# A streaming-encoder block on one core: turned inputs in alternating banks, weight units behind evictions and sums at two borders, one more warming matmul

## The chip, the cores and the metric

One core of one Trainium2 chip runs the whole program in one launch. The metric is the device time of that launch in microseconds, as the median of several runs.

## The reference

One layer (DEPTH is 1) on 256 tokens of width 1024, all in float32:

```python
x = x + 0.5 * rmsnorm(swiglu(rmsnorm(x, ffn1_pre_g), ffn1_w_in, ffn1_w_down), ffn1_post_g)
h = rmsnorm(x, mix_pre_g)
q_a, f_a, i_a, g_a, q_b, k_b, v_b, f_b, gates = split(h @ w_in)
y_a = (rmsnorm(hgrn2(q_a, f_a, i_a), hg_norm_g) * silu(g_a)) @ w_branch_a   # gated recurrence, 8 heads of 128
y_b = fox_attention(q_b, k_b, v_b, f_b + fox_f_bias) @ w_branch_b           # causal, with forget gates
y = sigmoid(gate_A) * y_a + sigmoid(gate_B) * y_b
x = x + rmsnorm(y @ w_out, mix_post_g)
x = x + rmsnorm(cross_attention(rmsnorm(x, mem_pre_g), rmsnorm(mem, mem_kv_g)) , mem_post_g)   # 4 heads, 256 memory rows
x = x + 0.5 * rmsnorm(swiglu(rmsnorm(x, ffn2_pre_g), ffn2_w_in, ffn2_w_down), ffn2_post_g)
```

`D_FF` is 2816. `rmsnorm(x, g)` is x divided by the root of its mean square, times a gain row.

## The kernel before

**Products in three parts.** Every projection keeps float32 accuracy by splitting both factors into a high part (rounded to the type `fp32r`) and a low part (what is left). A product is then hi times hi, hi times lo and lo times hi, added up in one PSUM bank. A matmul has 128 rows and mostly 512 columns.

**Weights in units.** The weights come from DRAM as units of 128 x 1024 floats (512 KB), in the order of `_ORDER`; `_AT[name] + i` is the number of unit i of a matrix. `unit(name, i)` loads one at its first use through `load_split`: SyncE issues the DMA into one of 4 `raw` buffers, ScalarE casts it to `hi` (L143), VectorE subtracts to get `lo` (L145), each into one of 8 buffers. Four units make one group of 512 columns (`chunk`); in a matrix laid out by rows (`mo`, `f2_dn`) each unit is one block of 128 rows. `place` gives a unit other buffers (named `w` in the profile: units 0 and 1 of `i_a` and of `f2_in`). `hold` names for a unit two instructions, one on ScalarE and one on VectorE: its cast is queued behind the first and its subtraction behind the second.

**The order of work.** The program is written once, in Python; a scheduler then puts each engine's instructions into a fixed queue, in the order of the program, but passing over what its own model says is not ready. Three means bind it: `hold`; `tc.issue_after(instruction)`, which queues what follows behind an instruction of the same engine; and `after(i)`, which puts TensorE work behind the i-th matmul of `log` (all matmuls so far) and ahead of everything else that is ready. Constants such as `L_MO` and `L_F2` are such places, counted from a mark `m = len(log)`.

**Turning.** Before each projection the tokens x (rows are tokens, `xs`, two halves of 128) are turned, so that the width lies on the partitions. `to_T` does this for one half: TensorE transposes eight blocks of 128 x 128 into two PSUM banks (four in each, from the pool `trp` of two banks), and `gain_split` evicts each block twice: ScalarE writes the high part with the gain (`hlT`, L358), VectorE the low part (L359), which needs the high one. `evicted` lists the two instructions of each block. `half` calls `to_T` for one half of the tokens, with all eight blocks at one mark or with four at each of two marks, and then `rstd_x` computes the half's 1/rms from sums of squares.

**After a projection.** `post` takes a half's two accumulators: sums of squares on ScalarE (`ssq`, junk), a reciprocal root in `root`, a scaled copy times the gain row on VectorE (`post`, L399), a refining `step`, and the sum into `xs` (L404).

**The two borders.** At border 1 the first FFN ends: its second half's last matmuls run while the first half is turned (mark `L_F1`), then `i_a`, the first projection of the mixer, starts: first half with column groups 0 and 1, then the second half (turned at `L_IA`). At border 2 the output projection `mo` of the cross-attention ends: `rows_proj(po[0], ...)`, `post(po[0])`, `rows_proj(po[1], ...)`, meanwhile the turning of the first half at `L_MO` and four matmuls later, then `post(po[1])`, and the second FFN starts with column groups 0 and 1 of `f2_in` for the first half; the second half is turned at `L_F2`.

**The start.** `WARM` float32 matmuls of ones by ones run while the first inputs (`head`, `raw`) are on their way; then `act_first` takes two column groups of FFN 1 together, block by block of the width as the inputs land.

**`mem_out`** multiplies the attention weights with the memory's values, two heads' columns at a time, into a bank of `trp`; the other pools of banks are `mm` (two) and `acc` (four).

Of the kernel before, what the change touches and what calls it, by code (L numbers as in the profile page):

```python
# [14 lines left out]
AF = mybir.ActivationFunctionType  # L15
ALU = mybir.AluOpType
AX = mybir.AxisListType

P = 128
# [17 lines left out]
L_F1 = 24  # L37
L_IA = 40
L_WO = 20
L_MK = 76  # L40
L_MO = 19
L_F2 = 36
L_OA = (4, 24)
F_S = 12
# [10 lines left out]

HX = T + 2 * KB

WARM = 7

X_AT = 12  # L60

# [8 lines left out]
_AT = {}  # L70
# [8 lines left out]
def block_kernel(ctx: ExitStack, tc: tile.TileContext, wts, head_in, gf_in, x_in, mem_in, memT_in, cols, rows, fbias, masks, out):  # L79
    nc = tc.nc  # L80
    V, S, G, PE = nc.vector, nc.scalar, nc.gpsimd, nc.tensor
# [21 lines left out]
    def nm(s):  # L103
        count[0] += 1
        return f"{s}_{count[0]}"
# [4 lines left out]
    def s1(n=1, dt=F32, name="s"):  # L110
        return sp.tile([P, n], dt, tag=f"s{n}", name=nm(name), bufs=16)
# [4 lines left out]
    def mm():  # L116
        return pp.tile([P, 512], F32, tag="mm", name=nm("mm"), bufs=2)

    def trp():
        return pp.tile([P, 512], F32, tag="tr", name=nm("tr"), bufs=2)  # L120
# [5 lines left out]
    evicted = []  # L126
    hold = {}
# [121 lines left out]
    ident = cp.tile([P, P], F32, name="ident")  # L249
# [9 lines left out]
    G_F1, G_MIX, G_MEM, G_KV, G_F2, G_HG, C_LB = 0, 8, 16, 24, 32, 40, 48  # L259
# [22 lines left out]
    def ssq(dst, src):  # L282
        S.activation(junk[:, : src.shape[-1]], src, AF.Square, accum_out=dst)  # L283
# [6 lines left out]
    def sums_of(s, pre2=None):  # L290

        b = s1(name="v")
        if pre2 is None:
            V.tensor_scalar(out=b, in0=s[:, 0:1], scalar1=D * EPS, scalar2=None, op0=ALU.add)
        else:
            V.tensor_scalar(out=b, in0=s[:, 0:1], scalar1=pre2, scalar2=D * EPS, op0=ALU.mult, op1=ALU.add)
        return b

    def root(s, b, pre=None, pre2=None):

        sc = 1.0 if pre2 is None else pre2
        y, v = s1(name="y"), s1(name="v")
        S.activation(y, s[:, 1:2], AF.Abs_reciprocal_sqrt, bias=b, scale=sc)
        S.activation(v, s[:, 1:2], AF.Identity, bias=b, scale=sc)
        z = y
        if pre is not None:
            z = s1(name="z")
            S.activation(z, y, AF.Copy, scale=pre)
        return y, v, z

    def step(y, v, z):
# [25 lines left out]
    def fac_of(i, h):  # L337
        return fac[i][:, 32 * h : 32 * h + 1]
# [14 lines left out]
    def gain_split(X, kb, src, g, a=0, b=T, first=False):  # L353
        gs = cols_s[:, g + kb : g + kb + 1] if isinstance(g, int) else g
        if first:
            hi = V.tensor_scalar(out=X.hi(kb, a, b), in0=src, scalar1=gs, scalar2=None, op0=ALU.mult)
        else:
            hi = S.activation(X.hi(kb, a, b), src, AF.Copy, scale=gs)  # L358
        lo = V.scalar_tensor_tensor(out=X.lo(kb, a, b), in0=src, scalar=gs, in1=X.hi(kb, a, b).bitcast(F32), op0=ALU.mult, op1=ALU.subtract)  # L359
        evicted.append((hi.ins, lo.ins))  # L360

    def to_T(X, src, h, g, qs=(0, 1)):

        for q in qs:
            ps = trp()
            for j in range(4):
                kb = 4 * q + j
                PE.transpose(ps[:, j * P : (j + 1) * P], src(kb), ident)  # L368
            for j in range(4):
                gain_split(X, 4 * q + j, ps[:, j * P : (j + 1) * P], g, h * P, h * P + P)  # L370

    def x_blocks(h):
        return lambda kb: xs[:, h, kb * P : (kb + 1) * P]
# [5 lines left out]
    def load_row(i):  # L379
        r = m4([P, D], n="grow")  # L380
        nc.sync.dma_start(r, rows[i].partition_broadcast(P))
        return r

    def post(ps, h, grow, factor=1.0, pre=None, cuts=((0, 512), (512, 1024)), store=False):

        pre2 = None
        if pre is not None:
            pre2 = s1(name="pre2")
            V.tensor_tensor(out=pre2, in0=pre, in1=pre, op=ALU.mult)
        s = s1(2, name="ss2")  # L390
        ts = []
        for j in range(2):
            ssq(s[:, j : j + 1], ps[j])
            if j == 0:
                b = sums_of(s, pre2)
            else:
                y = root(s, b, pre, pre2)
            t = sp.tile([P, 512], F32, tag="z2", name=nm("post"), bufs=3)
            V.scalar_tensor_tensor(out=t, in0=ps[j], scalar=-factor * 16.0, in1=grow[:, j * 512 : (j + 1) * 512], op0=ALU.mult, op1=ALU.mult)  # L399
            ts.append(t)  # L400
        r = step(*y)
        for a, b in cuts:
            xh = xs[:, h, a:b]
            V.scalar_tensor_tensor(out=xh, in0=ts[a // 512][:, a % 512 : (b - 1) % 512 + 1], scalar=r, in1=xh, op0=ALU.mult, op1=ALU.add)  # L404
            if store:
                (nc.scalar if a in (320, 768) else nc.sync).dma_start(out[h * P : (h + 1) * P, a:b], xh)


    def ffn(w_in, w_dn, X, r2, n_tok, i_row, first_half, second_half=None):
# [77 lines left out]
        for h in range(2):  # L487
            m = len(log)
# [5 lines left out]
        accs = None  # L494
        done = 0
        if callable(r2):
            outs = act_first((0, 1), acc)
            r2 = r2()
# [6 lines left out]
        for c in range(n_tok, NFF):  # L505
# [13 lines left out]
            if c == 6:  # L519
                grow = load_row(i_row)  # L520
# [3 lines left out]
            if accs is None:  # L524
                accs = [[acc(), acc()], [acc(), acc()]]
# [8 lines left out]
        m = len(log)  # L534
# [4 lines left out]
        m = len(log)  # L539
        if first_half:  # L540
            for c in range(NFF - STAG, NFF):
                down(c, 1)
            first_half(m)
            post(accs[1], 1, grow, 0.5, r2[1])
        else:
            for cut in (left, right):
                for c in range(NFF - STAG, NFF):
                    down(c, 1, (cut,))
            post(accs[1], 1, grow, 0.5, r2[1], ((0, 320), (320, 512), (512, 768), (768, 1024)), True)
# [4 lines left out]
    X1 = Joined()  # L554
    heads, raw1 = [], []
    for kb in range(KB):
# [7 lines left out]
        if kb % 2 == 0 or kb == 1:  # L564
            a, b = ((0, 512), (512, D))[kb] if kb < 2 else (0, D)
# [4 lines left out]
    one = nc.const_aps.tensor(1.0, (P, P), F32)  # L570
    for _ in range(WARM):
        MM(wps[:, :P], one, one, start=True, stop=True)
# [23 lines left out]
    X2 = Joined()  # L596
    r2 = [None, None]

    def half(X, r, h, g, *ms, into=None, act=True):

        for i, m in enumerate(ms):
            with after(m):
                to_T(X, x_blocks(h), h, g, (i,) if len(ms) == 2 else (0, 1))
        r[h] = rstd_x(x_halves(h), into, act)

    ffn("f1_in", "f1_dn", X1, norm_1, 0, 0, lambda m: half(X2, r2, 0, G_MIX, m + L_F1, into=fac_of(0, 0)))


    for i in range(2):
# [2 lines left out]
    for h in range(2):  # L612
        m = len(log)
        for c in range(2):
            ps = mm()
            if h == 0 and c == 1:
                for i in range(4):
                    hold[_AT["i_a"] + 4 + i] = evicted[-1 if i else -3]
            u = chunk("i_a", c)
            proj_tok(ps, X2, u, h)  # L620
            iv_last = S.activation(iv[c][:, h, :], ps, AF.Copy, scale=r2[h]).ins
        if h == 0:
            half(X2, r2, 1, G_MIX, m + L_IA, into=fac_of(0, 1))
# [25 lines left out]
    for c in range(2):  # L649
        u = chunk("f_a", c)  # L650
        f, k = m4([P, 2, 4, P], n="f"), m4([P, 2, 4, P], n="k")
        for j in range(2):
            fj = heads_of(f, j)
            for i in (2 * j, 2 * j + 1):
                ps = acc()
# [10 lines left out]
    for c in range(2):  # L666
        u = chunk("q_a", c)
        q = m4([P, 2, 4, P], n="q")
        for j in range(2):
            qj = heads_of(q, j)  # L670
            z = sp.tile([P, 2, 2, P], F32, tag="z2", name=nm("z2"), bufs=3)
            for i in range(2):
                ps = acc()
# [162 lines left out]
    for c in range(3):  # L836
        u = [load_split(gf_in[4 * c + i], GF) for i in range(4)]
        n = min(GF, D - c * GF)
        for h in range(2):
            ps = mm()  # L840
# [33 lines left out]
    for c in range(2):  # L874
        for name, lst, sc in (("k_b", kb_, 1.0), ("q_b", qb_, 1.0 / math.sqrt(128.0))):
            u = chunk(name, c)
            t = m4([P, 4, T], n=name)
            m = len(log)
            for j in range(2):
                if c == 0:  # L880
                    ps = proj_col2(X2, u, (2 * j, 2 * j + 1))
                else:
                    for i, bank in enumerate((mm, trp)):
                        ps = bank()
                        proj_both(ps, X2, u, 2 * j + i)
                        added(t[:, 2 * j + i], ps)
                    ps = t[:, 2 * j : 2 * j + 2]
# [32 lines left out]
    for h in range(2):  # L920
        ps = [acc(), acc()]
        for hd in range(8):
            g, i = hd // 4, hd % 4
# [5 lines left out]
        r = rstd_x(ps)  # L929
# [80 lines left out]
    m = len(log)  # L1010
    for c in range(2):
        u = chunk("v_b", c)
        t = m4([P, 2, 512], n="v_b")
        for h in range(2):
            ps = mm()
# [23 lines left out]
    m = len(log)  # L1039
# [43 lines left out]
    for c in range(2):  # L1083
        for name, X, zc in (("br_a", OA, c), ("br_b", OB, 2 + c)):
            u = chunk(name, c)
            for h in range(2):
                z = zs[zc][:, h]
                m = len(log)
                ps = mm()
# [21 lines left out]
    po = [[acc(), acc()], [acc(), acc()]]  # L1111
    m = len(log)
# [6 lines left out]
    m = len(log)  # L1119
# [5 lines left out]
    m = len(log)  # L1125
    for c in range(2):
        u = chunk("mk", c)
        KM.more()
        for j in range(2):
            js = slice(2 * j, 2 * j + 2)  # L1130
            t = sp.tile([P, 2, T], F32, tag="z2", name=nm("km"), bufs=3)
            for i in range(2):
                ps = acc()
# [6 lines left out]
    for c in range(2):  # L1140
        u = chunk("mq", c)
        QM.more()
        for i in range(4):
            ps = acc()
# [18 lines left out]
    m = len(log)  # L1163
# [39 lines left out]
    g3 = load_row(2)  # L1203
    AO = Pair()

    def mem_out(i):
        ps = trp()
        for j in range(2):
            o = ps[:, j * T : (j + 1) * T]
            for sb in range(2):  # L1210

                n = sb * 512 + (2 * (i % 2) + j) * P
                vh = VM.h[i // 2][:, n // T, n % T : n % T + P]
                vl = VM.l[i // 2][:, n // T, n % T : n % T + P]
                MM(o, vh, pT.h[sb][:, i], start=(sb == 0), stop=False)
                MM(o, vl, pT.h[sb][:, i], start=False, stop=False)
                MM(o, vh, pT.l[sb][:, i], start=False, stop=(sb == 1))
        i2 = slice(2 * (i % 2), 2 * (i % 2) + 2)
        marks[2 + i] = split(AO.h[i // 2][:, i2], AO.l[i // 2][:, i2], ps.rearrange("p (a t) -> p a t", a=2))
# [8 lines left out]
    for i in range(2, 4):  # L1228
        mem_out(i)
# [7 lines left out]
    po = [[acc(), acc()], [acc(), acc()]]  # L1237
# [2 lines left out]
            rows_proj(po[h], AO, "mo", h, (kb,))  # L1240
    for n in range(2):
        rows_proj(po[0], AO, "mo", 0, range(3, KB), (n,))
    post(po[0], 0, g3)
    m = len(log)
    rows_proj(po[1], AO, "mo", 1, range(3, KB))
    half(X4, r4, 0, G_F2, m + L_MO, m + L_MO + 4, into=fac_of(3, 0))
    post(po[1], 1, g3)


# [95 lines left out]
```

## Time and profile before

| | |
|---|---|
| median of 3 runs | 786.16 us (785.62 to 787.29) |
| the profiled execution | 788.36 us, of which its span is 786.1 us |
| TensorE (PE) busy | 777.3 us, 99% |
| VectorE (DVE) busy | 555.4 us, 71% |
| ScalarE (ACT) busy | 462.8 us, 59% |
| GpSimd (POOL) busy | 15.7 us, 2% |
| DMA | 148.08 MB, mean 188 GB/s |

How to read it: times count from the span's start. A row of the timeline is: start, length, engine, line, operation, what is written from what, shapes, how many merged into the row, and in brackets the idle time before it with what ended that. A row of waits is: who waited for whom, total us, times, longest. A row of the windows view is: stretch, its length, then for PE, PEld, DVE, ACT and POOL the busy time and the number of instructions, then the granted TensorE clock, the DMA share and GB/s. PE is TensorE's matmuls (their ends are modelled), PEld its weight loads; a tile's name stands without its number.

### The profile page before, as it was taken

The numbers are of one execution on the slowest core, as the hardware profiler recorded it, in microseconds if no ns is written. First come the engines' busy times: TensorE is split into PE (matmuls) and PEld (weight loads), VectorE is DVE, ScalarE is ACT, GpSimd is POOL, SyncE is SP. The second block draws the span as 40 slices with busy tenths as digits, with TensorE's granted clock in tenths as the row PEclk, the third lists the DMA queues.
The fourth block names the chain that finished last, engine by engine and source line by source line (L and its number), as shares of the span: only waits on it lengthen the run. The fifth ranks groups of instructions, "written<-read, shape, count | busy, mean of one in ns | idle before, by whom it ended". The sixth has DMA issues, their size and how long they took to land.

```text
span 786.1 us, 12160 instructions
## 1 busy us (share of the span) xinstructions
PE 777.3 (99%) x4620; PEld 669.9 (85%) x4620; DVE 555.4 (71%) x895; ACT 462.8 (59%) x777; POOL 15.7 (2%) x39
## 2 busy tenths in 40 slices
PE   9999999999999999999999999999999999999996
PEld 7888888888888999898888888888887888888885
DVE  7766665586778899588676666885588566655563
ACT  7664544566765668467676345753667554544552
POOL 0000000000000102100000000000000000000000
PEclk9999999999999999999999999999999999999999
DMA  9665665463654546734576655465174546665431
GB/s 347 245 223 202 228 211 207 161 211 125 216 205 145 181 135 208 276 122 152 183 263 226 215 181 168 148 207 181 54 263 166 166 163 203 217 211 199 161 108 53
DMA packets 44505, 148.08 MB, mean 188 GB/s; under 512 B 5144, under 2 KB 8864, under 8 KB 44448
## 3 DMA queue, kind: packets, MB, share of 16 engines
q1 hardware_dynamic: 43168, 144.83, 53.5%
q0 software_dynamic: 848, 2.12, 1.1%
q8 instruction: 36, 0.59, 0.3%
q10 hardware_dynamic: 432, 0.37, 0.2%
q14 instruction: 21, 0.17, 0.1%
HBM read 146.24 MB, written 1.06 MB: 187 GB/s over the span
## 4 chain that ended last, share of the span: by engine, by line
PE 95%; DMA 2%; ACT 1%; DVE 1%; issue 0%; DVEq 0%; ACTq 0%
PE mm L93 43%; PE acc L93 37%; PE tr L93 13%; DMA raw<-in_wts_dram 2%; PE tr L368 1%; ACT hi L143 1%; DVE lo L145 0%; DMA head<-in_head_dram 0%; PE tr L985 0%; PE tr L426 0%; PE tr L1079 0%; PE acc L1198 0%; DVE xs L404 0%; ACT junk L283 0%; DVE post L399 0%
## 5 line engine op out<-in xcount | busy, mean ns | idle before, releaser
L145 DVE TENSOR_TENSOR lo<-raw,hi 128x1024 fp32r<-128x1024 f32 (+1 forms) x252 | 299.2, 1203 | 70.1 <-ACT hi L143 44.9
L143 ACT CAST hi<-raw 128x1024 fp32r<-128x1024 f32 (+1 forms) x252 | 254.9, 1037 | 68.0 <-PE mm L93 33.4
L93 PE MATMUL mm<-hi,hlT 128*128 128x512 f32 (+1 forms) x480 | 143.8, 379 | 0.0
L93 PE MATMUL acc<-hi,act 128*128 128x512 f32 x352 | 111.2, 390 | 0.0
L93 PEld LDWEIGHTS mm<-hi,hlT 128*128 128x128 f32 x480 | 88.1, 188 | 14.6 <-DVE hlT L359 0.3
L93 PE MATMUL mm<-hlT,hi 128*128 128x512 f32 (+1 forms) x432 | 99.5, 360 | 0.0
L93 PE MATMUL mm<-lo,hlT 128*128 128x512 f32 (+1 forms) x240 | 89.5, 378 | 0.0
L93 PEld LDWEIGHTS mm<-hlT,hi 128*128 128x128 f32 x432 | 75.5, 189 | 10.6
L93 PEld LDWEIGHTS acc<-hi,act 128*128 128x128 f32 x352 | 66.2, 188 | 13.4
L93 PE MATMUL tr<-hlT,hi 128*128 128x512 f32 x288 | 72.1, 392 | 0.0
L93 PE MATMUL acc<-lo,act 128*128 128x512 f32 x176 | 68.8, 391 | 0.0
L93 PE MATMUL acc<-hlT,hi 128*128 128x512 f32 x272 | 68.4, 393 | 0.0
L93 PE MATMUL mm<-hlT,lo 128*128 128x256 f32 x368 | 60.9, 283 | 0.0
L93 PEld LDWEIGHTS tr<-hlT,hi 128*128 128x128 f32 x288 | 51.8, 189 | 9.3
L93 PEld LDWEIGHTS acc<-hlT,hi 128*128 128x128 f32 x272 | 48.9, 189 | 8.8
L93 PEld LDWEIGHTS mm<-hlT,lo 128*128 128x128 f32 x368 | 53.7, 190 | 3.0
L93 PEld LDWEIGHTS mm<-lo,hlT 128*128 128x128 f32 x240 | 45.0, 188 | 7.0
L215 ACT COPY plo<-mm 128x256 f32<-128x256 f32 x38 | 14.1, 372 | 55.0 <-PE mm L93 55.0
L93 PEld LDWEIGHTS tr<-hlT,lo 128*128 128x128 f32 x288 | 39.3, 190 | 2.8
L93 PE MATMUL tr<-hlT,lo 128*128 128x256 f32 x288 | 40.2, 282 | 0.0
L93 PEld LDWEIGHTS acc<-hlT,lo 128*128 128x128 f32 x272 | 37.3, 190 | 2.7
L93 PE MATMUL acc<-hlT,lo 128*128 128x256 f32 x272 | 38.6, 283 | 0.0
(245 smaller groups left out, 1002.1 us busy)
## 6 DMA issues: line engine op xcount, KB each, us to landing
raw<-in_wts_dram SPq DMA_DIRECT2D x247, 512.0 KB, 4.5
raw<-in_gf_dram SPq DMA_DIRECT2D x12, 344.0 KB, 3.9
head<-in_head_dram SPq DMA_DIRECT2D x7, 392.0 KB, 6.6
grow<-in_rows_dram SPq DMA_DIRECT2D x4, 512.0 KB, 6.9
xs<-in_x_dram SPq DMA_DIRECT2D x2, 512.0 KB, 7.7
cbm<-cd POOLq DMA_DIRECT2D x2, 512.0 KB, 8.4
brow<-in_rows_dram SPq DMA_DIRECT2D x4, 256.0 KB, 4.5
memT<-in_memT_dram SPq DMA_DIRECT2D x2, 512.0 KB, 5.8
```

The costliest lines, as they stand in the source:

```text
L93: log.append(PE.matmul(*args, **kw).ins)
L143: S.copy(h, r)
L145: V.tensor_tensor(out=l, in0=r, in1=h.bitcast(F32), op=ALU.subtract)
L215: S.copy(lo, ps[:, T:])
L368: PE.transpose(ps[:, j * P : (j + 1) * P], src(kb), ident)
```

## The change

Five edits:

- `to_T`, when it turns all eight blocks at once, puts the even blocks into one bank and the odd ones into the other, and evicts them in the order 0, 1, 2, ...; before, blocks 0 to 3 were in one bank and 4 to 7 in the other. With four blocks at a mark nothing changes.
- At border 1 units 6 and 7 of `i_a` are held behind the last instruction on ScalarE that `root` notes in the second half's `post` and behind its last sum on VectorE, no longer behind the last eviction.
- At border 2 unit 4 of `f2_in` is held behind the same two instructions of the first half's `post`, and units 6 and 7 behind the last eviction of the first half; `L_MO` goes from 19 to 15.
- `mem_out(2)` uses a bank of `mm`.
- `WARM` goes from 7 to 8.

```diff
--- before.py
+++ after.py
@@ -38,7 +38,7 @@
 L_IA = 40
 L_WO = 20
 L_MK = 76
-L_MO = 19
+L_MO = 15
 L_F2 = 36
 L_OA = (4, 24)
 F_S = 12
@@ -55,7 +55,7 @@
 
 HX = T + 2 * KB
 
-WARM = 7
+WARM = 8
 
 X_AT = 12
 
@@ -296,16 +296,20 @@
             V.tensor_scalar(out=b, in0=s[:, 0:1], scalar1=pre2, scalar2=D * EPS, op0=ALU.mult, op1=ALU.add)
         return b
 
+
+    rooted = []
+
     def root(s, b, pre=None, pre2=None):
 
         sc = 1.0 if pre2 is None else pre2
         y, v = s1(name="y"), s1(name="v")
         S.activation(y, s[:, 1:2], AF.Abs_reciprocal_sqrt, bias=b, scale=sc)
-        S.activation(v, s[:, 1:2], AF.Identity, bias=b, scale=sc)
+        last = S.activation(v, s[:, 1:2], AF.Identity, bias=b, scale=sc).ins
         z = y
         if pre is not None:
             z = s1(name="z")
             S.activation(z, y, AF.Copy, scale=pre)
+        rooted.append(last)
         return y, v, z
 
     def step(y, v, z):
@@ -361,13 +365,16 @@
 
     def to_T(X, src, h, g, qs=(0, 1)):
 
+        blocks = []
         for q in qs:
             ps = trp()
             for j in range(4):
-                kb = 4 * q + j
-                PE.transpose(ps[:, j * P : (j + 1) * P], src(kb), ident)
-            for j in range(4):
-                gain_split(X, 4 * q + j, ps[:, j * P : (j + 1) * P], g, h * P, h * P + P)
+
+                kb = 4 * q + j if len(qs) == 1 else 2 * j + q
+                blocks.append((kb, ps[:, j * P : (j + 1) * P]))
+                PE.transpose(blocks[-1][1], src(kb), ident)
+        for kb, p in sorted(blocks, key=lambda b: b[0]):
+            gain_split(X, kb, p, g, h * P, h * P + P)
 
     def x_blocks(h):
         return lambda kb: xs[:, h, kb * P : (kb + 1) * P]
@@ -401,9 +408,10 @@
         r = step(*y)
         for a, b in cuts:
             xh = xs[:, h, a:b]
-            V.scalar_tensor_tensor(out=xh, in0=ts[a // 512][:, a % 512 : (b - 1) % 512 + 1], scalar=r, in1=xh, op0=ALU.mult, op1=ALU.add)
+            summed = V.scalar_tensor_tensor(out=xh, in0=ts[a // 512][:, a % 512 : (b - 1) % 512 + 1], scalar=r, in1=xh, op0=ALU.mult, op1=ALU.add)
             if store:
                 (nc.scalar if a in (320, 768) else nc.sync).dma_start(out[h * P : (h + 1) * P, a:b], xh)
+        return rooted[-1], summed.ins
 
 
     def ffn(w_in, w_dn, X, r2, n_tok, i_row, first_half, second_half=None):
@@ -541,7 +549,7 @@
             for c in range(NFF - STAG, NFF):
                 down(c, 1)
             first_half(m)
-            post(accs[1], 1, grow, 0.5, r2[1])
+            return post(accs[1], 1, grow, 0.5, r2[1])
         else:
             for cut in (left, right):
                 for c in range(NFF - STAG, NFF):
@@ -603,7 +611,7 @@
                 to_T(X, x_blocks(h), h, g, (i,) if len(ms) == 2 else (0, 1))
         r[h] = rstd_x(x_halves(h), into, act)
 
-    ffn("f1_in", "f1_dn", X1, norm_1, 0, 0, lambda m: half(X2, r2, 0, G_MIX, m + L_F1, into=fac_of(0, 0)))
+    summed = ffn("f1_in", "f1_dn", X1, norm_1, 0, 0, lambda m: half(X2, r2, 0, G_MIX, m + L_F1, into=fac_of(0, 0)))
 
 
     for i in range(2):
@@ -615,7 +623,7 @@
             ps = mm()
             if h == 0 and c == 1:
                 for i in range(4):
-                    hold[_AT["i_a"] + 4 + i] = evicted[-1 if i else -3]
+                    hold[_AT["i_a"] + 4 + i] = summed if i > 1 else evicted[-1 if i else -3]
             u = chunk("i_a", c)
             proj_tok(ps, X2, u, h)
             iv_last = S.activation(iv[c][:, h, :], ps, AF.Copy, scale=r2[h]).ins
@@ -1204,7 +1212,7 @@
     AO = Pair()
 
     def mem_out(i):
-        ps = trp()
+        ps = mm() if i == 2 else trp()
         for j in range(2):
             o = ps[:, j * T : (j + 1) * T]
             for sb in range(2):
@@ -1240,10 +1248,13 @@
             rows_proj(po[h], AO, "mo", h, (kb,))
     for n in range(2):
         rows_proj(po[0], AO, "mo", 0, range(3, KB), (n,))
-    post(po[0], 0, g3)
+
+    hold[_AT["f2_in"] + 4] = post(po[0], 0, g3)
     m = len(log)
     rows_proj(po[1], AO, "mo", 1, range(3, KB))
     half(X4, r4, 0, G_F2, m + L_MO, m + L_MO + 4, into=fac_of(3, 0))
+    for i in (6, 7):
+        hold[_AT["f2_in"] + i] = evicted[-1]
     post(po[1], 1, g3)
 
 
```

## The prediction

> **What bounds the kernel now.** I read the page first, then TensorE's waits, then TensorE's timeline where those waits lie, then ScalarE's and VectorE's timelines there.
>
> ```profile
> span 786.1 us, 12160 instructions
> PE 777.3 (99%) x4620; PEld 669.9 (85%) x4620; DVE 555.4 (71%) x895; ACT 462.8 (59%) x777; POOL 15.7 (2%) x39
> PE acc L93 <- ACT hi L582: 0.6, 1, 0.6
> PE mm L93 <- ACT hlT L358: 0.4, 1, 0.4
> PE mm L93 <- DVE hlT L359: 0.2, 1, 0.2
> ```
>
> TensorE is busy for 777.3 of 786.1 us: it is the bound. The change removes no TensorE work (it adds one warming matmul), so it can only win back time in which TensorE stands still or runs slowly. The waits are few: 0.6 us at the start, and 0.4 and 0.2 us for `hlT`, the turned inputs. Busy time hides more, because a matmul's end is modelled; the spacing of starts shows it. A steady 512-column matmul starts 0.227 us after the last one (a row of two reads 0.62, one alone 0.39). I therefore look for larger spacings at the three places that the diff touches.
>
> **Border 2, memory attention to the second FFN.** TensorE, then ScalarE, then VectorE:
>
> ```profile
> 590.79 0.60 PE L368 MATMUL tr<-ident,xs 128*128 128x128 f32 x4
> ...
> 593.99 0.62 PE L93 MATMUL mm<-w,hlT 128*128 128x512 f32 x2
> 594.82 0.50 PE L93 MATMUL mm<-w,hlT 128*128 128x512 f32 x1 [0.21 <-DVE hlT L359]
> 595.70 0.73 PE L93 MATMUL mm<-w,hlT 128*128 128x512 f32 x2 [0.38 <-ACT hlT L358]
> ...
> 596.96 0.62 PE L93 MATMUL mm<-hi,hlT 128*128 128x512 f32 x2
> 597.54 0.73 PE L93 MATMUL mm<-w,hlT 128*128 128x512 f32 x2
> ```
> ```profile
> 585.70 1.04 ACT L143 CAST hi<-raw 128x1024 fp32r<-128x1024 f32 x1
> 586.64 0.59 ACT L283 ACTIVATE junk<-acc 128x512 f32<-128x512 f32 x1
> ...
> 590.64 1.03 ACT L143 CAST hi<-raw 128x1024 fp32r<-128x1024 f32 x1
> ...
> 592.21 1.03 ACT L143 CAST hi<-raw 128x1024 fp32r<-128x1024 f32 x1
> 593.14 0.36 ACT L358 ACTIVATE hlT<-tr,cols_s 128x128 fp32r<-128x128 f32 x1
> ```
> ```profile
> 587.05 1.22 DVE L145 TENSOR_TENSOR lo<-raw,hi 128x1024 fp32r<-128x1024 f32 x1
> 588.18 0.69 DVE L399 SCALAR_TENSOR_TENSOR post<-acc,grow 128x512 f32<-128x512 f32 x1
> ...
> 589.23 1.41 DVE L404 SCALAR_TENSOR_TENSOR xs<-post,y,xs 128x512 f32<-128x512 f32 x2
> ```
>
> Excess spacing, start to start less 0.227: into 594.82 (from 594.22, the second of its row) 0.37; into 595.70, 0.66; inside that row (0.73 where 0.62 is steady) 0.11; into 597.54 (from 597.19) 0.12; inside it 0.11. Sum 1.37 us. Its cause stands in the two lower fences. The transposes finish at 591.39, but the first eviction of the block runs on ScalarE only at 593.14, behind two weight casts (590.64 and 592.21). Counting casts back from the first placed unit, these are units 6 and 7 of `f2_in`; the cast at 585.70 is unit 4, and its subtraction is the 587.05 row, between the two halves of `post`.
>
> What the edits do here. Unit 4 goes behind `post`: its 1.22 us leave VectorE's queue ahead of the 588.18 row, and 1.04 us leave ScalarE's ahead of the 586.64 row. I work the new order from the same durations: second half of `post` done about 587.75, the two sums about 588.9 and 589.6, some 1.0 us earlier than now (589.98 and 590.64). `L_MO` from 19 to 15 puts the transposes four matmuls sooner: 590.79 less 4 times 0.227 is 589.88, after the sums, so TensorE does not wait there; were the sums not earlier, it would wait 0.1 us. Units 6 and 7 go behind the last eviction, so the first one starts near 590.4 instead of 593.14. Eviction of one bank is serial, one block per 0.78 us (next fence), so four take 3.1 us: blocks 0 to 3 by about 593.5, blocks 4 to 7 (in the other bank, transposed later by four matmuls and four transposes, 1.4 us) by about 594.9. TensorE wants block k at 593.99 plus 0.68 k. All arrive first: the 1.37 us go.
>
> What is queued behind the new waits: units 6 and 7 are cast and subtracted (1.03 and 1.22 us each) after 594.9 and are wanted by the second column group's blocks 4 to 7, 36 matmuls after 593.99, at 602.2. The raw buffer that unit 4 held is freed later by some 2.6 us (subtraction ending near 590.9, not 588.27), and those of 6 and 7 by several; SyncE's next loads into them slip by as much, but they feed the third group, 96 matmuls after 593.99, near 616. I cost these at nothing.
>
> **Border 1, first FFN to the mixer**, and the turned inputs:
>
> ```profile
> 188.24 0.37 ACT L358 ACTIVATE hlT<-tr,cols_s 128x128 fp32r<-128x128 f32 x1 [1.33 <-PE tr L368]
> 189.02 0.37 ACT L358 ACTIVATE hlT<-tr,cols_s 128x128 fp32r<-128x128 f32 x1 [0.42 <-DVE hlT L359]
> ...
> 193.27 1.23 DVE L145 TENSOR_TENSOR lo<-raw,hi 128x1024 fp32r<-128x1024 f32 x1
> ...
> 195.86 0.35 DVE L359 SCALAR_TENSOR_TENSOR hlT<-tr,cols_s,hlT 128x128 fp32r<-128x128 f32 x1
> ...
> 195.99 0.39 PE L93 MATMUL mm<-lo,hlT 128*128 128x512 f32 x1
> 196.26 0.73 PE L93 MATMUL mm<-hi,hlT 128*128 128x512 f32 x2
> ...
> 204.59 1.21 PE L93 MATMUL mm<-w,hlT 128*128 128x512 f32 x4
> ```
>
> ScalarE's eviction of block 1 sits idle 0.42 us until VectorE has read block 0 from the same bank: 0.78 us a block. With neighbours in two banks ScalarE reads one while VectorE reads the other, near 0.4 us a block, and blocks come in the order in which the next matmuls use them. Eight blocks from 188.24 end near 191.5 to 192, where now the last ends at 196.21. That removes the 0.05 and 0.11 us around 196.26, and in the second half's blocks the excess in the 204.59 row (1.21 less 0.39 less three times 0.227: 0.14). Together 0.30 us. `i_a` units 6 and 7 now wait for the sums, which come sooner than today without the 1.23 us subtraction ahead of them; their subtractions follow the sums today already, so that wait costs nothing. The same order in the two other blocks of eight (the recurrence's output, and the second half ahead of FFN 2) shows no excess beyond that of the transposes: nothing either way.
>
> **One bank.** `mem_out(2)` takes an `mm` bank, so `mem_out(3)` gets the transpose bank that is freed first.
>
> ```profile
> 568.79 0.40 PE L93 MATMUL acc<-lo,hT 128*128 128x512 f32 x1
> 569.07 0.39 PE L93 MATMUL tr<-hT,hT 128*128 128x256 f32 x1
> 569.29 0.28 PE L93 MATMUL tr<-hT,lT 128*128 128x256 f32 x1
> 569.41 0.28 PE L93 MATMUL tr<-lT,hT 128*128 128x256 f32 x1
> ```
>
> The excess is 0.05 us into 569.07, and 0.10 behind it (0.22 where 0.12 is steady). At most 0.15 us; below nothing only if the `mm` bank were occupied, and its eviction was long past. GpSimd's queue is not touched by any edit.
>
> **Warming.**
>
> ```profile
> 0.79 3.33 PE L93 MATMUL tr<-const-float32-1.0 128*128 128x128 f32 x14 [0.79 <-PEq L1334]
> 4.69 2.08 PE L93 MATMUL acc<-hi,hlT 128*128 128x512 f32 x4 [0.57 <-ACT hi L582]
> ...
> 7.40 0.50 ACT L358 ACTIVATE hlT<-head 128x256 fp32r<-128x256 f32 x1
> 7.42 1.79 PE L93 MATMUL acc<-hi,hlT 128*128 128x512 f32 x4
> ...
> 8.13 0.48 DVE L359 SCALAR_TENSOR_TENSOR hlT<-head,hlT 128x256 fp32r<-128x256 f32 x1
> ...
> 9.51 1.07 PE L93 MATMUL acc<-hi,hlT 128*128 128x512 f32 x4
> ```
> ```profile
> 2.10:5.52 3.42, 2.85 (x12) 2.46 (x12) 1.48 (x3) 1.63 (x4) 0.00 (x0) 1.00 0.94 292
> 5.52:8.93 3.41, 3.41 (x9) 2.64 (x9) 2.10 (x4) 2.13 (x5) 0.00 (x0) 1.00 1.04 406
> ```
>
> Until about 8.9 us matmuls run at half speed: four in 1.79 us are some 0.4 apart, four from 9.51 are 0.227 apart (1.07 less 0.39, by three). The clock column reads 1.00 throughout, so I go by the spacing. Seven warming calls are 14 matmuls in 3.33 us, some 0.22 apart (the last one's tail of about 0.4 left out); an eighth fills 0.44 of the 0.57 us of idle before 4.69 and delays nothing. Its worth lies between nothing and an earlier full speed. In the row pair, a stretch of 3.41 us without a gap came before the switch, and one with 2.85 busy of 3.42 did not bring it. With the gap at 0.13 us, 3.29 of 3.42 would be busy, between the two. If that suffices and speed rises near 5.5, the next limit is the input: block 1 is cast at 7.90 and its low part at 8.61, so its matmuls start near 7.95 and not 9.51, lose 0.25 on the low part, and 1.3 us stay, all later inputs being ahead. I take nothing, as the gap does not close entirely.
>
> The Trainium skill (TensorE: Matmul & The Clock Gate, Part 1) says that the clock is halved until one free-running window of about 3.4 us was busy, and gives no share that counts as busy. Read as wholly busy, it gives no gain, as I forecast; read as nearly so, it gives the first rival.
>
> **The sum.** 1.37, 0.30 and 0.15 are 1.82 us at most. I take off 0.3 for leftovers, since the first blocks arrive with under a microsecond to spare and the queues' order is newly made: 1.5. The profiled execution took 788.36 us (2.3 beside its span), the three timed ones 785.62 to 787.29; I subtract from the median, 786.16, giving 784.7 us. A difference of 0.2%, 1.6 us (784.6 to 787.7), is about what can be told from none.
>
> **Rivals.** (1) The warming counts too: 1.5 and 1.3 off, 783.4. For it: the gap left is a quarter of the old one. Against: no row shows that a partly idle stretch is enough. (2) The cover is gone behind border 2, which makes it slower: units 6 and 7 now compete with the second half's `post`, whose sums end today at 602.28 (601.54 and 0.74 long).
>
> ```profile
> 601.54 0.74 DVE L404 SCALAR_TENSOR_TENSOR xs<-post,y,xs 128x512 f32<-128x512 f32 x1
> 603.79 1.03 PE L368 MATMUL tr<-ident,xs 128*128 128x128 f32 x8
> ```
>
> The transposes that read them stand at 603.8 today and move up to 602.4 if 1.37 us are won. If both subtractions (2.44 us) land ahead of the sums, these end at 604.7 and TensorE waits 2.3 us: 0.8 more than was won, 787.0. It decides once the sums come over 1.5 us later than now. Against: VectorE is rid of eight evictions by then. (3) The change does not do what it says: unit 5 and later ones, which no new wait holds, slip between the evictions (each 1.0 to 1.2 us), and the stalls stay, 786.2.
>
> **How the numbers follow.** Forecast 0.42, rival (1) 0.36, (2) 0.10, (3) 0.12. The range runs from rival (1) with the whole 1.82 and a little more, 782.8, to rival (2), 787.1. The forecast lies on the border of what can be told: of its 0.42 I count 0.18 as faster, 0.24 as same; of rival (1) 0.34 faster, 0.02 same; rival (3) same; of rival (2) 0.06 slower, 0.04 same. Faster 0.52, same 0.42, slower 0.06.
>
> **What would show it.** Right: no TensorE idle row for `hlT`, spacing 0.227 from the first `mm<-w` on, transposes near 589.9 on today's scale, block 0's eviction ahead of units 6 and 7, `hlT` pairs 0.4 us apart at border 1. Rival (1): 0.227 spacing before 8.9. Rival (2): idle before the second half's eight transposes. Wrong altogether: new idle rows on TensorE away from these places.

## The result and the profile after

The changed kernel takes 784.84 us (median of 20 runs, 784.24 to 786.61), the kernel before 786.44 (20 runs beside it, 785.62 to 788.08). The ratio is 0.998, interval 0.9974 to 0.9986: 1.60 us faster, where 784.7 and 1.5 us were forecast. The profiled execution took 784.82 us, of which its span is 782.7; the span before was 786.1. That pair differs by 3.4 us, the medians by 1.6; the difference between the two is the point of half of what follows.

The page and then TensorE's waits of the kernel after:

```profile
span 782.7 us, 12158 instructions
PE 775.3 (99%) x4622; PEld 670.1 (86%) x4622; DVE 555.5 (71%) x895; ACT 462.9 (59%) x777; POOL 15.7 (2%) x39
```
```profile
PE tr L93 <- PEq L1345: 0.8, 1, 0.8
```

The waits for `hlT` are gone, and so is the 0.6 us for the first input; what is left is the program's own start.

**Border 2 after.** TensorE, ScalarE and VectorE in the timeline (L375 is the transposes, L362 and L363 the high and low parts, L406 `post`, L411 the sums):

```profile
587.89 0.60 PE L375 MATMUL tr<-ident,xs 128*128 128x128 f32 x4
...
589.26 0.60 PE L375 MATMUL tr<-ident,xs 128*128 128x128 f32 x4
...
592.00 2.88 PE L93 MATMUL mm<-w,hlT 128*128 128x512 f32 x12
594.72 0.39 PE L93 MATMUL mm<-hi,hlT 128*128 128x512 f32 x1
...
600.39 1.03 PE L375 MATMUL tr<-ident,xs 128*128 128x128 f32 x8
```
```profile
588.89 0.35 ACT L362 ACTIVATE hlT<-tr,cols_s 128x128 fp32r<-128x128 f32 x1
...
594.52 0.37 ACT L362 ACTIVATE hlT<-tr,cols_s 128x128 fp32r<-128x128 f32 x1 [0.34 <-DVE hlT L363]
594.78 2.00 ACT L143 CAST hi<-raw 128x1024 fp32r<-128x1024 f32 x2
```
```profile
586.29 1.41 DVE L411 SCALAR_TENSOR_TENSOR xs<-post,y,xs 128x512 f32<-128x512 f32 x2
587.62 1.22 DVE L145 TENSOR_TENSOR lo<-raw,hi 128x1024 fp32r<-128x1024 f32 x1
...
588.82 1.22 DVE L145 TENSOR_TENSOR lo<-raw,hi 128x1024 fp32r<-128x1024 f32 x1
589.95 0.35 DVE L363 SCALAR_TENSOR_TENSOR hlT<-tr,cols_s,hlT 128x128 fp32r<-128x128 f32 x1
...
595.51 0.35 DVE L363 SCALAR_TENSOR_TENSOR hlT<-tr,cols_s,hlT 128x128 fp32r<-128x128 f32 x1
595.77 0.74 DVE L411 SCALAR_TENSOR_TENSOR xs<-post,y,xs 128x512 f32<-128x512 f32 x1
```

Twelve matmuls in 2.88 us are 0.39 and eleven times 0.227: no excess, where before it was 1.37. The sums are done at 587.70, 0.2 us ahead of the transposes; the first eviction is 3.11 us ahead of the first `mm<-w` (0.85 before); units 6 and 7 are cast behind the last one. The holds act on VectorE too. Before, TensorE's first wait there (into 594.82) was ended by VectorE's low part of block 0, which stood behind the subtraction of unit 7:

```profile
593.27 1.23 DVE L145 TENSOR_TENSOR lo<-raw,hi 128x1024 fp32r<-128x1024 f32 x1 [0.30 <-ACT hi L143]
594.42 0.35 DVE L359 SCALAR_TENSOR_TENSOR hlT<-tr,cols_s,hlT 128x128 fp32r<-128x128 f32 x1
```

**Border 1 after**, TensorE, ScalarE, VectorE:

```profile
189.92 2.88 PE L93 MATMUL mm<-w,hlT 128*128 128x512 f32 x12
...
201.71 2.88 PE L93 MATMUL mm<-w,hlT 128*128 128x512 f32 x12
```
```profile
187.16 2.38 ACT L362 ACTIVATE hlT<-tr,cols_s 128x128 fp32r<-128x128 f32 x6 [1.33 <-PE tr L375]
189.44 1.04 ACT L143 CAST hi<-raw 128x1024 fp32r<-128x1024 f32 x1
```
```profile
187.56 2.36 DVE L363 SCALAR_TENSOR_TENSOR hlT<-tr,cols_s,hlT 128x128 fp32r<-128x128 f32 x6 [1.09 <-ACT hlT L362]
...
191.65 0.60 DVE L363 SCALAR_TENSOR_TENSOR hlT<-tr,cols_s,hlT 128x128 fp32r<-128x128 f32 x2
```

Six blocks in 2.38 us are 0.40 a block, on both engines at once, with idle only ahead of the first; before it was 0.78 a block. The last two blocks stand behind a weight cast (189.44) and its subtraction, and the eighth is done at 192.25.

**The bank**, TensorE's timeline: the spacing into the group is 0.28 us where 0.23 is steady, and then 0.22 where 0.12 is steady. That is 0.15 us, as before.

```profile
567.64 0.40 PE L93 MATMUL acc<-hi,hT 128*128 128x512 f32 x1
567.92 0.39 PE L93 MATMUL mm<-hT,hT 128*128 128x256 f32 x1
568.14 0.28 PE L93 MATMUL tr<-hT,hT 128*128 128x256 f32 x1
```

The weight load (PEld) of the late matmul shows what it waited for, before and then after, each under the row that ended its wait:

```profile
568.32 0.69 DVE L164 TENSOR_TENSOR lT<-tr,hT 128x512 fp32r<-128x512 f32 x1 [1.66 <-ACT hT L163]
569.07 0.19 PEld L93 LDWEIGHTS tr<-hT,hT 128*128 128x128 f32 x1 [0.32 <-DVE lT L164]
```
```profile
567.17 0.69 ACT L1168 ACTIVATE hT<-mm,facs 128x512 fp32r<-128x512 f32 x1
567.91 0.19 PEld L93 LDWEIGHTS mm<-hT,hT 128*128 128x128 f32 x1 [0.31 <-ACT hT L1168]
```

Before, it was VectorE's last reading of the transpose bank (`lT`, L164 is in `split`); after, it is the high part of the memory's values, which ScalarE writes for these products (L1168, in `mem_v`).

**The start**, TensorE's timeline:

```profile
0.79 3.75 PE L93 MATMUL tr<-const-float32-1.0 128*128 128x128 f32 x16 [0.79 <-PEq L1345]
4.44 2.08 PE L93 MATMUL acc<-hi,hlT 128*128 128x512 f32 x4
6.31 0.88 PE L93 MATMUL acc<-lo,hlT 128*128 128x512 f32 x2
7.02 1.07 PE L93 MATMUL acc<-hi,hlT 128*128 128x512 f32 x4
```

Full speed begins at 6.83, 2.1 us earlier than in the profile before (8.93); these moments are the first change of the granted clock in each trace. The first column groups end at 27.47 us, before at 28.55 (the end is counted as the start of the matmul that follows them).

**A place that the prediction did not look at**: the recurrence's 512 small matmuls. Before, then after:

```profile
268.28 0.23 PE L93 MATMUL acc<-qf,early 128*32 128x32 f32 x4
268.75 0.71 PE L93 MATMUL acc<-qf,early 128*32 128x32 f32 x58 [0.24 <-issue]
```
```profile
266.85 0.74 PE L93 MATMUL acc<-qf,early 128*32 128x32 f32 x62
```

Before, TensorE stands 0.44 us from start to start in the middle of the first burst (192 of the 512), waiting for nothing that the profile shows; after, not at all.

So the 3.4 us between the two profiles are: start 1.08, border 1 about 0.3, recurrence about 0.44, border 2 about 1.4, the bank 0, and under 0.2 elsewhere. The experiments say which of these the edits own.

### The profile page after: what moved, and what is told of

Same layout as the page of the kernel before. It is cut to its first block, busy times and chain, and to the rows that moved or that the text cites. A ratio compares the mean times of both kernels' runs of the same rounds, so it can differ in the third digit from the quotient of the medians.

```text
span 782.7 us, 12158 instructions
## 1 busy us (share of the span) xinstructions
PE 775.3 (99%) x4622; PEld 670.1 (86%) x4622; DVE 555.5 (71%) x895; ACT 462.9 (59%) x777; POOL 15.7 (2%) x39
## 4 chain that ended last, share of the span: by engine, by line
PE 99%; DVE 0%; issue 0%; DVEq 0%; ACT 0%; ACTq 0%
PE mm L93 43%; PE acc L93 40%; PE tr L93 14%; PE tr L375 1%; PE tr L993 0%; PE tr L434 0%; PE tr L1087 0%; PE acc L1206 0%; DVE xs L411 0%; DVE post L406 0%; DVEq L1351 0%; ACT junk L283 0%; DVE t L318 0%; PE tr L866 0%; DVE y L320 0%
```

## The experiments

Times are medians, or one time where there is one run; "excess" is worked as in the prediction, starts less 0.227 us. All edits but those to `WARM` 7, 9 and 1 are made on the kernel before.

**One warming matmul more, alone** (`e1_warm8`).

```diff
-WARM = 7
+WARM = 8
```

> The kernel before with the eighth warming matmul alone. My theory (the gain is TensorE's waits at the two borders): the same time as before, within 0.2 us in the median; border 2 keeps its 1.37 us of excess. Rival (the warming is worth as much as it was in the changed kernel's profile): 0.8 to 1.3 us faster in the median, 512-column matmuls 0.227 us apart from about 6 us on in most executions. The profiled execution alone cannot decide, since the moment of full speed may differ from one execution to the next; the median over five rounds decides.

786.57 us (11 runs) against 786.93 (35 runs), ratio 1.0001, 0.9992 to 1.0009: no difference that can be told. That excludes the rival's 0.8 us, but not a gain of 0.6. Full speed came at 6.37 us in its profile, though, and its first groups ended at 27.34. Its border 2, which no edit touches, has an excess of 0.55 us, not 1.37. One cast makes that difference; ScalarE before, then in this run:

```profile
584.17 1.05 ACT L143 CAST hi<-raw 128x1024 fp32r<-128x1024 f32 x1 [0.65 <-DMA raw<-in_wts_dram]
```
```profile
582.26 1.05 ACT L143 CAST hi<-raw 128x1024 fp32r<-128x1024 f32 x1 [0.40 <-DMA raw<-in_wts_dram]
```

Measured from the first matmul of `po[1]` (586.25 and 585.13), the load of this unit lands 0.8 us later in the profile before, and the casts ahead of the evictions with it. The five traces with the old border 2 (before, this run, and `e3_border1`, `e5_turn` and `e6_ia_wait` below) agree: the load lands 2.08, 2.86, 2.60, 2.05 and 2.15 us ahead of that matmul, and the excess is 1.37, 0.55, 0.80, 1.36 and 1.33. The size of border 2's stall thus goes with the moment at which a weight load lands. What I had expected, that border 2 keeps its 1.37, did not hold.

**The changed kernel with seven warming matmuls** (`e2_no_warm`).

```diff
-WARM = 8
+WARM = 7
```

> The changed kernel with seven warming matmuls again. My theory: 1.4 to 1.9 us faster than before, as the changed kernel (1.6 over all runs). Rival: 0.3 to 0.8 us faster, the rest having gone with the eighth warming matmul.

785.00 us, ratio to before 0.9982 (0.9972 to 0.9991), 1.4 us: the other edits carry the gain, or most of it. Three of its 11 runs lie over 786 (786.20, 786.75, 787.89); of the 20 of the changed kernel one does.

**Border 1 alone: the new order of turning and the new wait** (`e3_border1`).

```diff
+                kb = 4 * q + j if len(qs) == 1 else 2 * j + q
...
-                    hold[_AT["i_a"] + 4 + i] = evicted[-1 if i else -3]
+                    hold[_AT["i_a"] + 4 + i] = summed if i > 1 else evicted[-1 if i else -3]
```

> The kernel before with the alternating banks and the new wait of units 6 and 7 of i_a, nothing else. My theory: 0.3 us faster (the excess at 196 and 204.6 us goes), border 2 as before with about 1.4 us of excess. Rival (alternating banks also serve border 2, whose second half is turned that way): 1 us or more, with the excess at border 2 below 0.7.

786.29 us, ratio 0.9989 (0.9980 to 0.9997). Border 1 has no excess, border 2 0.80, and the stall in the recurrence is gone. The 0.3 us that I expected lie in the interval (0.2 to 1.6 us). The 0.80 fits neither side; the order of turning is not its cause, since the first half at border 2 is turned with four blocks at a mark, which the edit leaves alone.

**Border 2 alone: the three holds and the earlier transposes** (`e4_border2`).

```diff
-L_MO = 19
+L_MO = 15
...
-    post(po[0], 0, g3)
+    hold[_AT["f2_in"] + 4] = post(po[0], 0, g3)
...
+    for i in (6, 7):
+        hold[_AT["f2_in"] + i] = evicted[-1]
```

> The kernel before with the new waits of units 4, 6 and 7 of f2_in and L_MO 15, nothing else. My theory: 1.3 to 1.5 us faster, the excess at border 2 gone, that at border 1 (0.16 and 0.14) still there. Rival (the borders need each other, or the warming made the gain): under 0.8 us.

786.40 us, ratio 0.9992 (0.9983 to 1.0002): a median that can't be told from before, where I expected 1.3 to 1.5 us less. Yet its trace has no excess at border 2. Its 12 times stand in two groups, 785.00 to 785.84 and 786.97 to 787.55, six in each, and the profiled execution (787.42) is one of the second. There TensorE's start reads

```profile
4.77 2.06 PE L93 MATMUL acc<-hi,hlT 128*128 128x512 f32 x4 [0.66 <-ACT hi L587]
6.63 1.05 PE L93 MATMUL acc<-lo,hlT 128*128 128x512 f32 x2
7.49 1.91 PE L93 MATMUL acc<-hi,hlT 128*128 128x512 f32 x4
9.20 0.94 PE L93 MATMUL acc<-lo,hlT 128*128 128x512 f32 x2
```

with half speed up to 9.87 us and first groups ending at 29.02, 1.55 later than after. By its trace the border was won, and this execution lost it again at the start. That the two groups are early and late starts is not shown: the only profile is of the slower group.

**The new order alone, and the new wait at border 1 alone** (`e5_turn`, `e6_ia_wait`).

```diff
+                kb = 4 * q + j if len(qs) == 1 else 2 * j + q
```
```diff
-                    hold[_AT["i_a"] + 4 + i] = evicted[-1 if i else -3]
+                    hold[_AT["i_a"] + 4 + i] = summed if i > 1 else evicted[-1 if i else -3]
```

> The kernel before with the alternating banks alone. Its own theory (serial reading of one bank made border 1 late): the excess of 0.16 us near 196 and of about 0.11 near 204 goes to under 0.05. Rival (the weight subtractions between the evictions made it late, and only the new wait helps): at least 0.1 us stays near 196. On the 0.43 us in which TensorE stands at the recurrence's small matmuls near 268 us: it stood with the old border 1 in all three executions (0.43, 0.45, 0.54) and stood 0, 0 and 0.17 with the new one; if the turned order alone is the cause, it is under 0.2 here.

> The kernel before with units 6 and 7 of i_a behind the sums, blocks of a bank in the old order. Serial-bank theory: the excess near 196 and 204 stays at 0.16 and 0.11. Rival (the wait is what helps): it falls under 0.05. The 0.43 us near 268 should stay if it hangs on the turned order.

786.32 and 787.89 us, against 787.75 for one run of before. TensorE at the same place of border 1, with the order alone and then with the wait alone:

```profile
195.54 0.39 PE L93 MATMUL mm<-lo,hlT 128*128 128x512 f32 x1
195.76 0.61 PE L93 MATMUL mm<-hi,hlT 128*128 128x512 f32 x2
```
```profile
195.49 0.39 PE L93 MATMUL mm<-lo,hlT 128*128 128x512 f32 x1
195.76 0.73 PE L93 MATMUL mm<-hi,hlT 128*128 128x512 f32 x2
```

With the wait alone the old excess stays (0.05 into the row, 0.11 inside it); with the order alone it is gone, and that of the second half too (twelve matmuls in 2.88 us from 201.66 on). By these two traces the order does it all. The recurrence's stall is 0 with the order alone and 0.39 with the wait alone, as expected.

**Border 2's parts.** The three holds with `L_MO` left at 19 (`e7_waits_lmo19`: the first two edits), `L_MO` alone (`e8_lmo15`: the third), the hold of units 6 and 7 alone (`e11_units67`: the second), that of unit 4 alone (`e12_unit4`: the first).

```diff
+    hold[_AT["f2_in"] + 4] = post(po[0], 0, g3)
...
+    for i in (6, 7):
+        hold[_AT["f2_in"] + i] = evicted[-1]
...
-L_MO = 19
+L_MO = 15
```

> The three new waits at border 2 with L_MO still 19. Theory (the waits win it, the place of the transposes is only room): excess at border 2 at most 0.2 us, the last low part of the eight blocks some 0.9 us later against the first matmul of the second FFN than with L_MO 15. Rival (the place wins it): 0.5 us or more of excess.

> L_MO 15 alone, no new waits. Theory: TensorE waits 0.1 to 0.3 us at the first transposes, since the sums are not there, and the first eviction still runs behind two casts: 0.5 to 1.4 us of excess at border 2 as in three executions with the old one (1.37, 0.55, 0.80). Rival: under 0.3 us.

> The kernel before with units 6 and 7 of f2_in behind the last eviction, unit 4 free, L_MO 19. The prediction's step (the two casts ahead of the first eviction cost most): the excess at border 2, 1.37, 0.55, 0.80, 1.36 and 1.33 us in five executions without any of the new waits, falls to 0.3 or less. Rival (the late sums of post cost most): 0.5 or more stays.

> The kernel before with unit 4 of f2_in behind post, units 6 and 7 free, L_MO 19. The prediction's step: sums about 1.0 us earlier against the first matmul of the second half's output projection (4.4 us after it now), but the first eviction still behind the two casts: 0.4 us or more of excess stays. Rival (the late sums cost most): 0.3 or less.

Single times are 785.80, 787.65, 787.19 and 786.80 us, too few for a difference of this size; the traces tell them apart. TensorE with units 6 and 7 held, then with unit 4 held:

```profile
594.36 2.89 PE L93 MATMUL mm<-w,hlT 128*128 128x512 f32 x12
```
```profile
593.01 1.53 PE L93 MATMUL mm<-w,hlT 128*128 128x512 f32 x6
594.38 0.40 PE L93 MATMUL mm<-hi,hlT 128*128 128x512 f32 x1
595.25 0.96 PE L93 MATMUL mm<-w,hlT 128*128 128x512 f32 x3 [0.47 <-ACT hlT L362]
596.05 0.40 PE L93 MATMUL mm<-lo,hlT 128*128 128x512 f32 x1
596.34 0.74 PE L93 MATMUL mm<-w,hlT 128*128 128x512 f32 x2
```

The excess is 0 with the holds of all three, 0 with that of 6 and 7 alone, 0.93 with unit 4's alone (0.64 into 595.25), 0.54 with `L_MO` alone. Without the hold of units 6 and 7 some excess stays in every trace, and with it there is none: that hold is the gain.

Two things limit this. The load whose landing sets the size of the stall came earliest of all fourteen traces in the run with units 6 and 7 alone (3.12 us ahead of the first matmul of `po[1]`), so that run does not show that their hold is enough when the load is late. And unit 4's hold does something that no single time shows: in all seven traces with it the sums end 3.44 or 3.45 us after that matmul, wherever the load lands (2.10 to 2.91 ahead), and without it 3.44 to 4.42. The earlier transposes bring the first eviction forward (3.11 us ahead of the first `mm<-w`, against 2.56 with `L_MO` at 19), but not the last low part, 3.86 us after it against 3.84, where I had expected 0.9 of difference. Nor did TensorE wait at the transposes with `L_MO` alone, as I had expected: the sum that the first four read was done 0.5 us ahead of them.

**Nine warming matmuls, and one** (`e9_warm9`, `e10_warm1`), on the changed kernel.

```diff
-WARM = 8
+WARM = 9
```
```diff
-WARM = 8
+WARM = 1
```

> The changed kernel with nine warming matmuls, so that none of the idle time before the first inputs is left and the first matmul comes 0.1 to 0.3 us later. Clock theory (full speed comes at the end of one of a row of equal stretches, if the stretch was nearly all busy; where the rows begin differs between executions; the gap ahead of the first inputs spoils a stretch): full speed between 4.2 and 7.6 us in every execution, times as the changed kernel, 1.4 to 1.9 us below before, no execution over 1 us above the lowest. Rival (the moment of full speed does not depend on warming): some executions 1 us or more above the lowest, as with seven.

> The changed kernel with one warming matmul. Clock theory: the stretch must lie behind the first inputs, so full speed comes between 8 and 11.5 us in every execution, and the median is 0.9 to 1.8 us above the changed kernel's, that is from 0.7 us below to 0.2 us above before; the early times of seven warming matmuls (4.3 and 4.9 us to full speed) do not occur. Rival (warming is worth nothing): 1.4 to 1.9 us below before, as the changed kernel.

Nine: 784.73 us (6 runs, 784.29 to 785.47), ratio to before 0.9970 (0.9959 to 0.9981), about the time with eight, with full speed from 6.71 us. That is 2.4 us below before, more than the 1.4 to 1.9 expected, and one execution lies 1.2 us above the lowest, where I had expected none over 1 us. One: 789.39 us (8 runs), ratio to before 1.0029 (1.0018 to 1.0039). I had expected about the time of before or less, and missed by 2 us. Late full speed (9.29 us, first groups done at 28.68) accounts for 1.2 us of it. The rest stands in the recurrence; TensorE, then the windows:

```profile
268.06 0.33 PE L93 MATMUL acc<-qf,early 128*32 128x32 f32 x17
270.73 0.60 PE L93 MATMUL acc<-qf,early 128*32 128x32 f32 x45 [2.34 <-issue]
```
```profile
272.12:275.54 3.42, 3.42 (x14) 3.42 (x13) 1.57 (x5) 0.99 (x2) 2.47 (x12) 0.50 0.30 121
276.00:279.00 3.00, 3.00 (x21) 3.00 (x20) 2.27 (x5) 2.52 (x4) 0.00 (x0) 1.00 0.00 0
```

The stall that was 0.44 us before is 2.5 here, and from 272.12 to 275.54 the granted clock (the third number from the end) is 0.50, another 1.7 us. Together 5.3 us (1.2, 2.4 more stall than in the changed kernel, 1.7), as the spans differ: 788.0 and 782.7. I had not expected the last two. Seven of the eight executions have a mean granted clock of 0.995, and none of another kernel is below 0.997; the eighth has 0.999 and took as long (789.37), so what it paid in place of the half-speed stretch is open.

## Why the prediction was right, and where it was not

**Border 2: the mechanism held; the 1.37 was one execution's.** Held are the steps: sums 1.0 us earlier (3.44 us after the first matmul of `po[1]`, before 4.39), transposes 4.11 us ahead of the first `mm<-w` (589.88 against 593.99 was 4.11), no wait there, no excess. But kernels with the old border 2 show 1.37, 0.55, 0.80, 1.36 and 1.33, on average 1.08; the prediction took one profile's value for all.

**The last block's low part was mis-sized.** Blocks 4 to 7 were to be done 0.9 us after the first `mm<-w`; the last is done at 595.86, 3.86 after it. VectorE's queue holds what the working left out: units 4 and 5's subtractions ahead of the first low part (1.22 each), and between the low parts the second half's two products and a sum (0.68, 0.68 and 0.75). TensorE wants block 7 at 592.00 plus seven times 0.68, 596.76. That leaves 0.9 us to the block's first matmul: no stall, but the room is that thin.

**Border 1: right, but for the last two blocks.** 0.30 us were forecast; 0.27 (0.16 and 0.11) stand in all eight traces with the old order, none in those with the new. Eviction at 0.40 a block holds for the six blocks in one row, which have no idle between them. All eight were to be done 3.3 to 3.8 us after the first began; it took 5.09 (187.16 to 192.25), since the working left out the weight cast and subtraction ahead of the last two. Before it was 7.97, and TensorE did not need them sooner. The Trainium skill (PSUM — Partial Sum Buffer, PSUM bank collisions raise a hardware error) says that ScalarE and VectorE must not be in one bank at once, and that a dependency is put between two such instructions. The traces agree: before, ScalarE's 0.42 us of idle in front of block 1 was ended by VectorE's reading of block 0, and it goes when the banks alternate.

**The bank: 0.15 forecast at most, 0 measured.** The wait for a bank that was still being read was real (VectorE's reading ended at 569.01, the late matmul starts at 569.07). The edit removed it, and a wait that the working did not look for stands in its place: the values' high part is done at 567.86, and the matmul that needs it starts at 567.92. The change from 512 to 256 columns is not the cause: of 117 such changes in the profile before, this is the only one with over 0.24 us into it.

**Warming: costed at nothing, and not settled to better than 0.6 us.** Rival (1) was priced at 1.3 us and did show in the profile after (full speed at 6.83, the start 1.08 us shorter). In the median of the run with this edit alone it does not, since full speed is a matter of the execution. With seven warming matmuls it came between 4.26 and 4.92 us in five profiles, at 6.34 in one, and 8.93, 8.98, 9.87 and 10.31 in four; with eight or nine at 6.37, 6.71 and 6.83. An early full speed does not help much, as the inputs are not there yet, so the first groups' end is the better measure: on average 28.0 us in the ten traces with seven, 27.4 in the three with eight or nine.

The Trainium skill (TensorE: Matmul & The Clock Gate, Part 1) says that the window of about 3.4 us runs free of the kernel's start. The traces agree: the clock's changes within one execution lie on one grid (9.29 and 272.12 in the run with one warming matmul are 262.83 us apart, 77 times 3.413), and where that grid lies against the span's start differs between executions. The prediction took nothing because the gap ahead of the first input does not close entirely, and no row showed that a partly idle stretch is enough. The traces do show it. With seven warming matmuls the 3.41 us ahead of the switch to full speed were busy for 2.75 us in one profile and 2.96 to 3.26 in five; this is the windows view of `e2_no_warm`:

```profile
1.51:4.92 3.41, 2.96 (x14) 2.67 (x13) 0.82 (x3) 1.89 (x4) 0.02 (x1) 1.00 0.91 254
```

Stretches with the same gap in them and 2.71 to 2.85 us busy brought no switch in the four late ones. Of the two readings that the prediction gave, nearly busy fits and wholly busy does not. So the gap cost some executions a stretch of half speed and spared others, by where the grid lay; what share is enough stays open, as the ends of matmuls are modelled and about 2.75 us did in one profile and not in another. Three profiles with eight or nine are too few to say that early or late ones do not occur there.

**Rival (2), late sums of the second half, went the other way**: they end at 596.51, 3.9 us ahead of the transposes at 600.39, where they were 1.5 ahead before. **Rival (3), unit 5 and later in between**: unit 5 does stand ahead of the evictions, at no cost to TensorE. New idle rows elsewhere, which would have made the forecast wrong altogether, there are none.

**The sum: 1.5 came from 1.82 less 0.3 for leftovers.** The leftovers did not come, the bank gave nothing, and the recurrence's stall was missing. By the traces, typical values are 1.08 (border 2) and 0.27 (border 1), 1.35 together; the recurrence's stall was 0.44, 0.46, 0.54, 0.39, 0.37 and 0.40 us in six of the eight traces with the old order and none in two, and with the new order none in three, 0.18 and 0.28 in two (the run with one warming matmul left aside). That is 0.33 against 0.09 on average, 0.24 us, and the total 1.59, against 1.60 measured. That this agrees to 0.01 is luck: the start, 0.6 us by the same kind of average, is not in it, and the measured 1.60 is itself known to about 0.5 (1.1 to 2.0). The forecast was close partly because the misses cancel: border 2 and the bank 0.44 too large, the leftovers 0.3 and the recurrence 0.24 too small, and the start perhaps 0.6 too small. That the order of turning is what moves the recurrence's stall is not shown: it goes with the order in the traces, but what lies between is open.

## What to carry to other kernels

An eviction that the next matmuls wait for should not queue behind weight casts that are wanted much later: hold those behind the last eviction, and check the trace for the matmuls' spacing, as most of this stall was never counted as idle. ScalarE and VectorE read one bank in turn here, 0.78 us a block; alternating banks in the order of use gave twice the rate, 0.40, as long as no weight cast stood between. Before a stall from one profile is put into a sum, look whether its cause, here a load's landing, is steady: the same stall was 0.55 to 1.37 us. Where a wait is taken away, look for what the waiting instruction needs next, as at the bank.

## What was not expected of the hardware

**In a burst of tiny matmuls TensorE stood still at one place of its instruction stream, just after a packet of instructions had landed.** In nine of the fourteen traces it stands behind exactly 3009 of its recorded instructions (matmuls, weight loads and its sequencer's), whichever matmul of the burst that is: with more warming matmuls it is an earlier one, and with one warming matmul, which takes twelve matmuls out of the start, one twelve later. A packet of the "instruction" queue (q8 in the profile) lands shortly before. TensorE goes on 1.27 to 1.50 us after that landing in all nine. In the profile before it lands 0.35 us after the burst's start, and the stall is 0.44; with one warming matmul it lands 2.33 after it, and the stall is 2.54. Where it lands 0.20 us or more ahead of the start (four traces), there is no stall; of the three that land less than 0.20 ahead, one (0.03 ahead) has none either. That the landing releases the stall is read from this order; no run changed it by itself.

**Behind a stall of 2.3 us the clock was halved for 3.42 us.** The 3.41 us ahead of 272.12 hold 2.0 us of idle, and the stretch behind runs at 0.50. The stalls of 0.54 us and less had no such sequel. Where between them the limit lies no run here shows.
